# Retention's last gate behind the first Fourier projection, Fourier's second gate between later branches, and the first modulation in eight pieces

## The chip, the cores and the metric

The kernel runs on one core of one Trainium2 chip. The metric is the device time of one execution in microseconds (us). The engines are PE (TensorE, matrix products), DVE (VectorE), ACT (ScalarE), POOL (GpSimd) and SP (which only issues transfers); PEld is PE's weight load, and a q behind a name (SPq, ACTq) is the queue from which that engine issues transfers.

## The reference, cut to what matters

Two layers of a trunk on 640 tokens (512 of a sample, 128 of a prompt) of width 1024. Each layer modulates its input, projects it once into many strips, runs three branches, gates each with a SiLU of its own strip of the projection, multiplies each by a branch weight, merges the three under sigmoid gates, and projects back.

```python
mod = silu(cvec) @ w_mod + b_mod
shift, scale, gate = split(mod, 3)
h = rms_norm(x, norm_g) * (1 + scale) + shift
rq, rk, rv, rz, q_lat, kv_lat, k_r, mz, fu, fz, gl = split(h @ w_in)
o_r = head_norm(retention(rq, rk, rv))        # 4 heads of 128
o_m = mla_attend(q_lat, kv_lat, k_r)          # 8 heads
o_f = fft2(fu).real                           # 4 groups of 128
branches = stack([o_r * silu(rz), o_m * silu(mz), o_f * silu(fz)])
proj = einsum(branches, w_branch)             # 3 x (512 -> 1024)
merged = sum(proj * sigmoid(gl))              # gl: 3 x 1024 columns
x = x + gate * (merged @ w_out)
```

## The kernel before, in words

Hidden values lie transposed: channels on partitions, the 640 tokens along the row, so one strip of 128 channels is a tile of 128x640. Each float32 operand is split into a high and a low part (`split`, L78 the cast on ACT, L74 the difference on DVE or POOL), and each product takes three passes (high by high, low by high, high by low). `hh` and `hl` are the two parts of h; `wh` and `wl` those of a weight.

**Order.** A tile scheduler puts the instructions of each engine into one fixed order; the place of a statement in the code is its priority. At run time every engine works its list strictly in that order, and an instruction that waits holds up all behind it on that engine.

**Start** (L1150 to L1190). SP issues the loads: x in five tiles, then the columns of the modulation weight `w_mod` and four pieces of the weight of the latents (`lat_w`, tiles `raw` of 128x2x384) in the order of the string `m2 w0 m0 w1 n6 n2 n7 n3 w2 w3`: m is a block of 512 columns in two transfers of 1 MB, n one of 256 columns in two of 0.5 MB, all in the ring `mraw` of five buffers of 1 MB. PE multiplies a block by the conditioning (`fill`, L187), ACT copies the result (L192), PE turns it over (L196), and it lands in `modT`, the scale and shift. x is squared in 20 pieces on ACT (L1168), summed and rooted on DVE and POOL, spread (L245), turned over (L1178), scaled (L1181, `xr`), modulated (L1187) and split into `hh` and `hl`, for the eight channel blocks d = 0 to 7. Blocks 0 to 3 need m2 and m0, 4 and 5 need n6 and n2, 6 and 7 need n7 and n3. The latents (384 columns, 120 matmuls) come first, then the keys' and values' latents (288 columns, 120 matmuls).

**Retention** (L690 to L835). Head by head: scores, mixing, `norm(hd)` and `gate(hd)`. `norm` copies the head's output to a tile `of` (L782), turns it over (five transposes, L787), takes mean and variance (DVE L789, L790), a power on POOL (L793, L794), the offset on DVE (L795), and normalises on ACT (L798). `gate` turns it back (five transposes, L807) and multiplies by the SiLU of strip rz (DVE L808). The strips of rz are computed by `Filler` (L319, 48 matmuls a strip, with tanh L321 and DVE L322), which other work pours between its own instructions; `finish` pours what is left of a strip. `norm(3)` and `gate(3)` stand at the end.

**Fourier** (L838 to L945). `sums(0)` to `sums(3)` form sums of token halves of h (`hx`, `hq0h` and so on, the operands of `seven` below), using the tiles `of` as scratch. `project(g)` makes two groups of the projection fu in five products of 24 matmuls (`sm`, L85 to L87), each copied by ACT (`un`, L855, from a ring of `sm` banks). Transforms follow, and gates: `z0`, `z1` for the groups 0 and 1 (`fourier_gate`, L954), and behind them, in the branch part, groups 2 and 3 by one `seven`.

**Branches** (L1192 to L1310). `seven` computes 256 output columns with seven half-sized products (84 matmuls of 320 columns, L1109) instead of eight, from sums of inputs and sums of weights. The loop `n` takes the branches in the order attention, retention, Fourier; in each, i = 0 to 3 takes 256 columns of the sigmoid gate (a `seven` from `hq`), then of the branch product (a `seven` from `bq`, or `four`). The operands `bq0` to `bq9` and `bql` are parts of the branch's input, made by `branch_sums` with sums on DVE (L1010 to L1013) and splits, at the ticks of the first gate's `seven` or at once behind it. `bql` lies in the memory of the Fourier tiles `of`, so those are stored to `ofd` first and loaded back into `or` for the third branch; `om` holds attention's output and then scratch. `tick` also steers `steps`, the loads (`mraw`, by ACTq) and products of the next modulation.

## Time and profile before

| | us |
|---|---|
| device time, median of 3 runs (1477.54 to 1480.52) | 1479.51 |
| the profiled execution's own time | 1482.52 |
| its span in the trace | 1480.7 |
| PE busy in the span | 1416.7 (96%) |
| DVE busy | 1024.6 (69%) |
| ACT busy | 758.5 (51%) |
| POOL busy | 241.8 (16%) |

Times in the rows are microseconds from the start of the span. A row of the timeline gives the start, the busy time, the engine, the line and operation with the tile it writes and those it reads, how many follow in a row, and in brackets the idle time of the engine before it and what released it. Matmuls overlap, so a matmul of 0.31 us may be followed by the next one 0.15 us later. PEclk is the clock that TensorE was granted, 1.00 for 2.4 GHz; a stretch below 1.00 ran partly at 1.2 GHz. The chain that ended last is 72% PE, 13% DVE, 6% transfers, 4% ACT.

### The profile page before, as it was taken

What the parts mean: (1) busy time and instruction counts of PE and PEld (TensorE: products, weight loads), DVE (VectorE), ACT (ScalarE), POOL (GpSimd) and SP (SyncE); (2) the same over time, 40 slices, a digit from 0 to 9 for tenths busy, and PEclk for the clock granted to TensorE, in tenths of its full rate; (3) what the DMA queues carried; (4) which work ended last, traced back from release to release, by engine and by line L of the source; (5) the groups of instructions that cost most, each with busy time, mean ns of one, the idle gap of its engine ahead of it and who ended that gap; (6) DMA issues with size and microseconds to landing.
All of it is one profiled execution on the core that took longest, in us unless ns stands there. A gap on an engine that the chain in (4) does not pass through costs nothing.

```text
span 1480.7 us, 25121 instructions
## 1 busy us (share of the span) xinstructions
PE 1416.7 (96%) x9761; PEld 1346.9 (91%) x9761; DVE 1024.6 (69%) x1894; ACT 758.5 (51%) x1635; POOL 241.8 (16%) x227
## 2 busy tenths in 40 slices
PE   5999999999999999999999999999999999999997
PEld 3989989988897898999999899899889889999997
DVE  5367776667886686698573777765759768779843
ACT  6357666544544453455344566664545445445542
POOL 1220100301102111122312100021110112112240
PEclk9999999999999999999999999999999999999999
DMA  9520002421326464133532100042222424333342
GB/s 330 164 76 1 15 15 78 121 76 41 93 90 189 143 192 122 51 86 93 171 104 83 34 15 15 15 137 75 74 72 65 154 82 116 95 82 86 90 125 86
DMA packets 173735, 138.91 MB, mean 94 GB/s; under 512 B 8240, under 2 KB 164528, under 8 KB 173616
## 3 DMA queue, kind: packets, MB, share of 16 engines
q1 hardware_dynamic: 155568, 120.16, 28.0%
q10 hardware_dynamic: 18048, 17.15, 3.7%
q8 instruction: 77, 1.26, 0.4%
q14 instruction: 42, 0.34, 0.1%
HBM read 125.98 MB, written 11.30 MB: 93 GB/s over the span
## 4 chain that ended last, share of the span: by engine, by line
PE 72%; DVE 13%; DMA 6%; ACT 4%; issue 4%; POOL 1%; SPq 0%; POOLq 0%; DVEq 0%; ACTq 0%
PE bank L1109 25%; PE sm L85 5%; PE sm L87 5%; PE sm L86 5%; PE bank L1080 4%; PE big L513 4%; PE fill L319 3%; PE big L269 3%; PE sm L319 3%; PE sm L534 3%; DVE wl L74 2%; PE sm L526 2%; DMA mraw<-in_w_mod 2%; PE fill L187 1%; DMA raw<-in_w_in 1%
## 5 line engine op out<-in xcount | busy, mean ns | idle before, releaser
L74 DVE TENSOR_TENSOR wl<-raw,wh 128x1024 fp32r<-128x1024 f32 (+5 forms) x146 | 156.2, 1072 | 92.1 <-ACT wh L78 45.1
L78 ACT CAST wh<-raw 128x1024 fp32r<-128x1024 f32 (+5 forms) x126 | 104.4, 832 | 79.0 <-DMA raw<-in_w_in 18.1
L85 PE MATMUL sm<-wh,hh 128*128 128x256 f32 (+2 forms) x456 | 134.7, 296 | 0.4 <-DVE vl L74 0.4
L87 PE MATMUL sm<-wh,hl 128*128 128x256 f32 (+2 forms) x456 | 133.9, 294 | 0.9 <-DVE hl L74 0.9
L1109 PE MATMUL bank<-hh,wh 128*128 128x320 f32 x416 | 130.7, 316 | 4.0 <-ACT tg L1125 2.9
L86 PE MATMUL sm<-wl,hh 128*128 128x256 f32 (+2 forms) x456 | 134.5, 295 | 0.0
L1109 PE MATMUL bank<-hl,wh 128*128 128x320 f32 x416 | 129.5, 312 | 0.0
L1109 PE MATMUL bank<-hh,wl 128*128 128x320 f32 x416 | 127.8, 313 | 0.0
L74 POOL TENSOR_TENSOR wl<-raw,wh 128x1024 fp32r<-128x1024 f32 (+1 forms) x32 | 67.6, 2112 | 296.9 <-ACT wh L78 221.2
L74 POOL TENSOR_TENSOR wl<-st,wh 128x512 fp32r<-128x512 f32 x26 | 39.2, 1508 | 324.2 <-ACT wh L78 302.1
L85 PEld LDWEIGHTS sm<-wh,hh 128*128 128x128 f32 x456 | 88.2, 194 | 1.5 <-DVE vl L74 0.8
L87 PEld LDWEIGHTS sm<-wh,hl 128*128 128x128 f32 x456 | 88.0, 193 | 1.4 <-DVE hl L74 1.4
L86 PEld LDWEIGHTS sm<-wl,hh 128*128 128x128 f32 x456 | 88.4, 194 | 0.1
L1109 PEld LDWEIGHTS bank<-hh,wh 128*128 128x128 f32 x416 | 79.1, 190 | 9.9 <-ACT tg L1125 3.6
L1109 PEld LDWEIGHTS bank<-hl,wh 128*128 128x128 f32 x416 | 79.2, 190 | 0.0
L1109 PEld LDWEIGHTS bank<-hh,wl 128*128 128x128 f32 x416 | 78.7, 191 | 0.4 <-DVE raw L1025 0.4
L74 DVE TENSOR_TENSOR ptl<-sm,pth 128x384 fp32r<-128x384 f32 x128 | 67.4, 549 | 14.4 <-ACT pth L78 13.3
L1109 PE MATMUL bank<-bq,wh 128*128 128x320 f32 x320 | 72.1, 311 | 0.0
L78 ACT CAST pth<-sm 128x384 fp32r<-128x384 f32 x128 | 57.5, 480 | 24.1 <-PE sm L526 23.3
L78 ACT CAST wh<-st 128x512 fp32r<-128x512 f32 x68 | 39.7, 618 | 53.0 <-PE bank L1109 53.0
L640 DVE TENSOR_REDUCE nm<-big 128x1 f32<-128x768 f32 x64 | 60.7, 948 | 2.7 <-PE big L513 2.4
L74 DVE TENSOR_TENSOR wl<-st,wh 128x512 fp32r<-128x512 f32 x42 | 41.2, 980 | 30.2 <-ACT wh L78 27.7
(579 smaller groups left out, 4546.3 us busy)
## 6 DMA issues: line engine op xcount, KB each, us to landing
raw<-in_w_in SPq DMA_DIRECT2D x96, 512.0 KB, 4.0
mraw<-in_w_mod ACTq DMA_DIRECT2D x32, 512.0 KB, 4.3
raw<-in_w_branch SPq DMA_DIRECT2D x24, 512.0 KB, 3.6
raw<-in_w_out SPq DMA_DIRECT2D x16, 512.0 KB, 4.5
mraw<-in_w_mod SPq DMA_DIRECT2D x4, 1024.0 KB, 11.7
mraw<-in_w_mod SPq DMA_DIRECT2D x8, 512.0 KB, 8.3
raw<-in_w_in SPq DMA_DIRECT2D x8, 384.0 KB, 5.9
om<-xd SPq DMA_DIRECT2D x16, 192.0 KB, 3.1
```

Of the source, the lines that this page charges most:

```text
L74: eng.tensor_tensor(lo, src, hi.bitcast(F32), op=ALU.subtract)
L78: ACT.copy(hi, src)
L85: PE.matmul(out, ah, bh, start=first, stop=False)
L86: PE.matmul(out, ah, bl, start=False, stop=False)
L87: return PE.matmul(out, al, bh, start=False, stop=last)
L269: PE.matmul(ps[:, 512 * h:512 * h + 320], ws[a][:, k, :], xs[b][k][:, 320 * h:320 * h + 320], start=(first and k == 0 and i == 0), stop=(l ...
L319: PE.matmul(ps, w[a][:, k, :], (hh, hl)[b][k][:, hs], start=(k == 0 and i == 0), stop=(k == NK - 1 and i == 2))
L513: PE.matmul(S[:, 512 * h:512 * h + 384], qT[hd][a][:, t * P:(t + 1) * P], (kth, ktl)[b][hd % 3][:, 384 * h:384 * h + 384], start=(i == 0), ...
L534: PE.matmul(po[:, :256], vt[hd // 4][kt][:, hd % 4, :], pts[hd, qb][b][kt // 3][:, kt % 3, :], start=(kt == 0 and b == 0), stop=(kt == 5 a ...
L640: DVE.tensor_reduce(nm, Sv, axis=AX.XY if len(Sv.shape) == 3 else AX.X, op=ALU.max, negate=True)
L1080: PE.matmul(A, ws[u][:, k, j * P:(j + 1) * P], xs[k][v][:, h, :], start=(k == 0 and i == 0), stop=(k == 3 and i == 2))
L1109: PE.matmul(ps, w[u], x[v], start=(first and k == 0 and j == 0), stop=(k == n - 1 and j == 2), skip_group_check=True)
```

## The change

1. `retention` no longer runs `gate(3)` but returns it. `fourier` runs `sums(0)`, `project(0)`, then that gate, then `sums(1)` to `sums(3)`; before, the gate stood first, then the four sums, then `project(0)`. Head 3's normalised output lies in the last of the four `of` tiles, which `sums(1)` uses.
2. The gates of Fourier's groups 2 and 3 (columns `C_FZ+256`, one `seven` with its weights, two tanh, two SiLU products, two gates) move from behind the Fourier branch into the loop, ahead of n = 2. They are now applied in `or`, where the Fourier tiles have been loaded back. The weights that were fetched ahead for it (`w0`) are now those of the first gate of n = 0. All four stores to `ofd` are issued at the first tick of n = 0 (before: two behind Fourier, two behind the gates).
3. The first modulation comes in eight blocks of 256 columns, in the order 4, 0, w0, 5, 1, w1, 6, 2, w2, 7, 3, w3, in a ring of ten buffers of 0.5 MB, and the modulation of blocks d = 2i, 2i+1 is written right behind its two blocks. x is squared in five pieces of 1024 with the sum accumulated, ahead of the loads in the code.
4. In the branches the parts of `bq` change place in the list (`bql` serves the products 3 and 6, before 4 and 6), at n = 0 a part is made at every tick (before at every second), and the scratch tiles of n = 2 swap parity.

```diff
--- before.py
+++ after.py
@@ -832,10 +832,10 @@
         for p in todo:
             mix(*p)
         norm(3)
-        gate(3)
-
-
-    def fourier(l, fp, of, sums, wgp):
+        return lambda: gate(3)
+
+
+    def fourier(l, fp, of, sums, wgp, lastgate):
         def table(name, src, a, n):
             raw = fp.tile([P, a, n], F32, name="traw", tag="traw", bufs=1)
             nc.sync.dma_start(raw, src)
@@ -915,9 +915,11 @@
             split(upc[0][:, g, :], upc[1][:, g, :], Up[:, 0:P], scale=1.0 / 128)
             split(ups[0][:, g, :], ups[1][:, g, :], Up[:, P:256], scale=-1.0 / 128)
 
-        for k in range(4):
+        sums(0)
+        project(0)
+        lastgate()
+        for k in range(1, 4):
             sums(k)
-        project(0)
         teo = [table(f"te{i}", A["k_dft"][i].rearrange("(a p) n -> p a n", p=P), 2, 256) for i in range(2)]
         tp_ = table("tpr", A["k_dftp"].unsqueeze(1), 1, 256)
         cf = table("tcf", A["k_dftf"].unsqueeze(1), 1, 256)
@@ -938,7 +940,7 @@
         along_c(3)
         fourier_prompt(of, cf, upc, ups)
         wz, z1 = wload(rows(A["w_in"][l], 0, NK, C_FZ + P, P), NK, P, DVE), []
-        ws = gl_weights(wgp, l, C_FZ + 256, lambda: z1.append(silu2(l, C_FZ + P, wz)))
+        ws = gl_weights(wgp, l, C_GL + D, lambda: z1.append(silu2(l, C_FZ + P, wz)))
         fourier_gate(of, 0, z0)
         return ws, fourier_gate(of, 1, z1[0])
 
@@ -994,7 +996,7 @@
         B = lambda i, c: sv[:, i, :, HALF[c]]
         t = [gp.tile([P, 2, 320], F32R, name=f"bq{i}", tag=f"bq{i}", bufs=1) for i in range(10)]
         x = [spare[:, i, :].rearrange("p (k n) -> p k n", k=2) for i in range(4)]
-        t = t[:8] + x[:2] + t[8:] + x[2:]
+        t = t[:6] + x[:2] + t[6:] + x[2:]
 
         def place(i, x, eng):
             hi, lo = t[2 * i:2 * i + 2]
@@ -1149,25 +1151,17 @@
 
     po1 = sm()
 
-    def start(order):
-        for o in order.split():
-            if o[0] == "w":
-                first.append(lat_w(0, int(o[1])))
-            else:
-                n, b = {"m": 512, "n": 256}[o[0]], int(o[1])
-                for j in range(0, NK, 4):
-                    mod_use(0, b, j, mod_load(0, b, j, prep, n, 512, 4, 5, nc.sync), n, 4, po1[:, 2 * (b * n // P):])
+    def scaled(d):
+        v = xrs[d]
+        for c, s_ in ((0, slice(0, T)), (1, slice(T, TT))):
+            DVE.tensor_scalar(v[:, s_], v[:, s_], modT[0][:, 8 + d, c:c + 1], modT[0][:, d, c:c + 1], op0=ALU.mult, op1=ALU.add)
+        split(hh[d], hl[d], v, leng=POOL if d % 2 else DVE)
 
     for t in range(NT):
         nc.sync.dma_start(xn[t], A["x_sample"][0, t * P:(t + 1) * P, :] if t < 4 else A["x_prompt"][0])
-    start("m2 w0 m0 w1 n6 n2 n7 n3 w2 w3")
     rin = prep.tile([P, NT], F32, name="rin")
-    rq4 = prep.tile([P, NT, 4], F32, name="rq4")
     for t in range(NT):
-        for j in range(4):
-            ACT.activation(omt[:, j, 0:256], xn[t][:, 256 * j:256 * j + 256], AF.Square, scale=D ** -0.5,
-                           accum_out=rq4[:, t, j:j + 1])
-    DVE.tensor_reduce(rin, rq4, axis=AX.X, op=ALU.add)
+        ACT.activation(omt.rearrange("p w n -> p (w n)")[:, 0:D], xn[t], AF.Square, scale=D ** -0.5, accum_out=rin[:, t:t + 1])
     POOL.tensor_scalar(rin, rin, EPS, None, op0=ALU.add)
     POOL.tensor_tensor(rin, rin, mhalf[:, 0:NT], op=ALU.pow)
     R, _ = bcast(prep, rin, 0, NT)
@@ -1181,11 +1175,13 @@
         DVE.tensor_tensor(xr, ps[:, :TT], R, op=ALU.mult)
         xts.append(xt)
         xrs.append(xr)
-    for d in range(NK):
-        v = xrs[d]
-        for c, s_ in ((0, slice(0, T)), (1, slice(T, TT))):
-            DVE.tensor_scalar(v[:, s_], v[:, s_], modT[0][:, 8 + d, c:c + 1], modT[0][:, d, c:c + 1], op0=ALU.mult, op1=ALU.add)
-        split(hh[d], hl[d], v, leng=POOL if d % 2 else DVE)
+    for i in range(4):
+        for b in (4 + i, i):
+            for j in range(0, NK, 4):
+                mod_use(0, b, j, mod_load(0, b, j, prep, 256, 256, 4, 10, nc.sync), 256, 4, po1[:, 4 * b:])
+        first.append(lat_w(0, i))
+        for d in (2 * i, 2 * i + 1):
+            scaled(d)
     xstore = [nc.sync.dma_start(xd[0][d], xts[d]) for d in range(NK)]
     pre.close()
 
@@ -1202,18 +1198,16 @@
         orr = [ort[:, w, :] for w in range(4)]
         off = [oft[:, w, :] for w in range(4)]
         with ExitStack() as s:
-            retention(l, pool(s, f"re{l}"), orr, off)
+            lastgate = retention(l, pool(s, f"re{l}"), orr, off)
         s3 = ExitStack()
         hqp = pool(s3, f"hq{l}")
         wgp = pool(s3, f"wg{l}")
         with ExitStack() as sx:
             sums, close, hq = hidden_sums(hqp, pool(sx, f"hx{l}"), off)
             with ExitStack() as s:
-                w0, gated = fourier(l, pool(s, f"fo{l}"), off, sums, wgp)
+                w0, gated = fourier(l, pool(s, f"fo{l}"), off, sums, wgp, lastgate)
             close()
         ofd = dp.tile([P, 4, TT], F32, name=f"ofd{l}")
-        for w in range(2):
-            nc.sync.dma_start(ofd[:, w, :], oft[:, w, :])
         mgp = pool(s3, f"mg{l}")
         mg = [mgp.tile([P, TT], F32, name=f"mg{d}") for d in range(NK)]
         mh, ml = hh, hl
@@ -1226,16 +1220,13 @@
             steps = mod_steps(blocks, gp)
             next(steps)
             a, b = HALF
-            zs = [fl.tile([P, TT], F32, name="tg", tag="th", bufs=2) for _ in range(2)]
 
             def fourier_done(j):
-                z, m, o = zs[j], mg[j], off[j + 2]
+                z, m, o = om[2 + j], om[j], ort[:, 2 + j, :]
                 ACT.activation(m, z, AF.Tanh, scale=0.5)
                 DVE.scalar_tensor_tensor(m, m, 1.0, z, op0=ALU.add, op1=ALU.mult)
-                fourier_gate(off, j + 2, m)
-                nc.sync.dma_start(ofd[:, j + 2, :], o)
-
-            seven(w0, hq, *zs, lambda ps: ACT.copy(zs[0][:, b], ps), fourier_done, lambda i: None)
+                DVE.scalar_tensor_tensor(o, o, 0.5, m, op0=ALU.mult, op1=ALU.mult)
+
             bql = rp2.tile([P, 4, TT], F32R, name="bql", tag="of", bufs=1)
 
             def merge(d0, d1, hs=slice(0, TT)):
@@ -1253,7 +1244,10 @@
                 def tick(i):
                     if i in (3, 6):
                         next(steps, None)
-                    if i % 2 and len(bq) < np_:
+                    if not n and not bq and not i:
+                        for w in (2, 3, 0, 1):
+                            nc.sync.dma_start(ofd[:, w, :], oft[:, w, :])
+                    if (i % 2 or not n) and len(bq) < np_:
                         with tc.issue_after(gated.ins):
                             bq.append(next(parts))
 
@@ -1278,15 +1272,17 @@
             for n, (idx, src, tmp) in enumerate(((1, omt, None), (0, ort, om), (2, ort, om))):
                 if n:
                     flush()
+                if n == 2:
+                    seven(gl_weights(wgp, l, C_FZ + 256), hq, om[2], om[3], lambda ps: ACT.copy(om[2][:, b], ps), fourier_done, lambda i: None)
                 parts = branch_split(gp, src) if n == 1 else branch_sums(gp, src, bql)
                 np_ = 4 if n == 1 else 7
                 bq = []
                 for i in range(4):
-                    if n and i % 2 == 0:
+                    if n and i % 2 == n - 1:
                         y2 = tmp[2:4]
                     else:
                         y2 = [fl.tile([P, TT], F32, name="tg", tag="th", bufs=2) for _ in range(2)]
-                    seven(gl_weights(wgp, l, C_GL + D * idx + 256 * i), hq, *y2, *gates(y2, n, bq, parts, np_))
+                    seven(w0 if not (n or i) else gl_weights(wgp, l, C_GL + D * idx + 256 * i), hq, *y2, *gates(y2, n, bq, parts, np_))
                     if n == 2 and i == 3:
                         merge(0, 4)
                     if i == 0:
```

SP, the loads at the start, before (`mraw` 1 MB or 0.5 MB, `raw` 0.39 MB):

```order
L175 DMA mraw_188<-in_w_mod 128x4x512
L175 DMA mraw_195<-in_w_mod 128x4x512
L92 DMA raw_208<-in_w_in 128x2x384
L175 DMA mraw_214<-in_w_mod 128x4x512
L175 DMA mraw_221<-in_w_mod 128x4x512
L92 DMA raw_233<-in_w_in 128x2x384
L175 DMA mraw_239<-in_w_mod 128x4x256
L175 DMA mraw_246<-in_w_mod 128x4x256
L92 DMA raw_309<-in_w_in 128x2x384
L175 DMA mraw_257<-in_w_mod 128x4x256
```

and now:

```order
L175 DMA mraw_284<-in_w_mod 128x4x256
L175 DMA mraw_291<-in_w_mod 128x4x256
L175 DMA mraw_302<-in_w_mod 128x4x256
L175 DMA mraw_309<-in_w_mod 128x4x256
L92 DMA raw_319<-in_w_in 128x2x384
L175 DMA mraw_333<-in_w_mod 128x4x256
L175 DMA mraw_340<-in_w_mod 128x4x256
L175 DMA mraw_351<-in_w_mod 128x4x256
L175 DMA mraw_358<-in_w_mod 128x4x256
L92 DMA raw_368<-in_w_in 128x2x384
L175 DMA mraw_382<-in_w_mod 128x4x256
L175 DMA mraw_389<-in_w_mod 128x4x256
```

The large transfers are gone; two blocks of 256 columns stand ahead of each piece of the latents' weight.

ACT in the first layer, from the normalisation of head 3 (L798) to the copies of `project(0)` (L855), before (`wh` and `th` belong to the gates' strips and weights):

```order
L321 ACTIVATE th_4267<-fill_4268 128x320
L782 COPY of_2986<-big_4098 128x640
L78 CAST wh_4607<-raw_4605 128x1024
L321 ACTIVATE th_4267<-fill_4295 128x320
L798 ACTIVATE of_2986<-big_4233,nm5_4252,rs5_4251 128x128 x5
L855 COPY un_4404<-sm_4417 128x256
L855 COPY un_4404<-sm_4443 128x256
L855 COPY un_4404<-sm_4469 128x256
L78 CAST te0h_4552<-traw_4550 128x512
```

and now:

```order
L782 COPY of_3000<-big_4112 128x640
L321 ACTIVATE th_4466<-fill_4467 128x320
L798 ACTIVATE of_3000<-big_4247,nm5_4266,rs5_4265 128x128 x5
L78 CAST wh_4621<-raw_4619 128x1024
L321 ACTIVATE th_4466<-fill_4494 128x320
L855 COPY un_4314<-sm_4327 128x256
L855 COPY un_4314<-sm_4353 128x256
L855 COPY un_4314<-sm_4379 128x256
L78 CAST te0h_4566<-traw_4564 128x512
```

The weight cast and the tanh stand behind L798 instead of ahead of it, and ahead of the three copies.

PE at the same place, around the last gate's transposes (L807), before (`sm_4469` and `sm_4495` are the third and fourth product of `project(0)`):

```order
L85 MATMUL sm_4469<-wh_4413,hh7_156 128x256
L86 MATMUL sm_4469<-wl_4414,hh7_156 128x256
L87 MATMUL sm_4469<-wh_4413,hl7_164 128x256
L807 MATMUL big_4322<-ident_72,of_2986 128x128 x5
L85 MATMUL sm_4495<-wh_4407,hh0_149 128x256
L86 MATMUL sm_4495<-wl_4408,hh0_149 128x256
```

and now (`fill` is the gate strip's second half, `sm_4405` the fourth product of `project(0)`):

```order
L319 MATMUL fill_4494<-hh7_156,wh_4462 128x320
L319 MATMUL fill_4494<-hl7_164,wh_4462 128x320
L319 MATMUL fill_4494<-hh7_156,wl_4463 128x320
L807 MATMUL big_4521<-ident_72,of_3000 128x128 x5
L85 MATMUL sm_4405<-wh_4317,hh0_149 128x256
L86 MATMUL sm_4405<-wl_4318,hh0_149 128x256
```

The gate's transposes stand behind the strip's matmuls and ahead of the fourth product. Between L787 and L807 now stand 24 matmuls of the strip, before 1 of the strip and 23 of the third product.

DVE at the entry of n = 2 in the first layer, before (`bq` are the operands of the third branch, `wl` weights, `tg` and `om` results of `seven`):

```order
L1022 TENSOR_TENSOR st_7272<-raw2_7264 128x512
L74 TENSOR_TENSOR bq1_7052<-or_2985,bq0_7051 128x640
L74 TENSOR_TENSOR bq5_7056<-or_2985,bq4_7055 128x640
L1010 TENSOR_TENSOR or_2985<-or_2985 128x2x320
L74 TENSOR_TENSOR wl_7086<-raw_7061,wh_7085 128x1024
L74 TENSOR_TENSOR bq7_7058<-or_2985,bq6_7057 128x640
L1013 TENSOR_TENSOR or_2985<-or_2985 128x2x320
L74 TENSOR_TENSOR bq3_7054<-or_2985,bq2_7053 128x640
```

and now (`or` holds the Fourier tiles):

```order
L1227 SCALAR_TENSOR_TENSOR om_165<-om_165 128x640
L1115 TENSOR_TENSOR om_165<-bank_7004,om_165 128x320
L1228 SCALAR_TENSOR_TENSOR or_2999<-or_2999,om_165 128x640
L1227 SCALAR_TENSOR_TENSOR om_165<-om_165 128x640
L1228 SCALAR_TENSOR_TENSOR or_2999<-or_2999,om_165 128x640
L74 TENSOR_TENSOR wl_7279<-raw_7274,wh_7278 128x1024
L1115 TENSOR_TENSOR tg_7042<-bank_7148,tg_7042 128x320
L74 TENSOR_TENSOR bq9_7040<-or_2999,bq8_7039 128x640
L1026 TENSOR_TENSOR raw_7274<-raw_7274,raw2_7276 128x512
L1027 TENSOR_TENSOR raw_7274<-raw_7274,st_7285 128x512
L74 TENSOR_TENSOR bq5_7036<-or_2999,bq4_7035 128x640
L1010 TENSOR_TENSOR or_2999<-or_2999 128x2x320
```

The two SiLU products and the two gates stand ahead of the first operands of the branch, which before came with no gate ahead.

## Rows read from the trace of the kernel before

**Rows 1.** The page: PE's busy time.

```profile
PE 1416.7 (96%) x9761; PEld 1346.9 (91%) x9761; DVE 1024.6 (69%) x1894; ACT 758.5 (51%) x1635; POOL 241.8 (16%) x227
```

**Rows 2.** Waits of PE: line, waited for, us in total, times, longest.

```profile
PE fill L187 <- DMA mraw<-in_w_mod: 13.4, 4, 12.4
PE big L807 <- ACT of L798: 5.3, 2, 2.6
PE bank L1109 <- ACT bql L78: 4.1, 2, 2.1
PE bank L1109 <- ACT tg L1125: 2.9, 2, 2.4
```

**Rows 3.** Windows: busy us by engine, PEclk, DMA share, GB/s; around PE's waits.

```profile
380.00:385.00 5.00, 4.96 (x25) 4.46 (x26) 3.97 (x8) 3.82 (x11) 0.61 (x1) 0.67 0.84 218
465.00:470.00 5.00, 2.94 (x14) 1.90 (x15) 3.20 (x6) 3.96 (x7) 0.17 (x1) 0.71 0.81 261
1190.00:1195.00 5.00, 5.00 (x24) 5.00 (x25) 5.00 (x8) 2.47 (x6) 1.82 (x1) 0.66 0.02 6
```

**Rows 4.** Windows as above, of the start.

```profile
17.00:22.00 5.00, 4.99 (x31) 3.12 (x27) 1.69 (x2) 2.98 (x5) 0.29 (x1) 1.00 1.05 386
27.00:32.00 5.00, 3.78 (x39) 2.50 (x37) 4.89 (x12) 3.64 (x8) 0.00 (x0) 1.00 1.10 357
61.00:77.00 16.00, 16.00 (x118) 16.00 (x117) 2.47 (x7) 10.48 (x30) 7.46 (x18) 1.00 0.16 46
```

**Rows 5.** Timeline of the start.

```profile
7.17 0.42 ACT L1168 ACTIVATE om<-xn 128x256 f32<-128x256 f32 x1 [2.49 <-DMA xn<-in_x_sample]
...
39.25 0.33 PE L86 MATMUL sm<-wl,hh 128*128 128x384 f32 x1
...
39.94 0.34 PE L87 MATMUL sm<-wh,hl 128*128 128x384 f32 x1
...
77.14 0.60 PE L403 MATMUL sm<-ident,latq 128*128 128x128 f32 x4
```

**Rows 6.** Timeline of the last norm and gate of retention, first layer.

```profile
373.05 0.71 PE L787 MATMUL big<-ident,of 128*128 128x128 f32 x5
373.25 1.05 ACT L78 CAST wh<-raw 128x1024 fp32r<-128x1024 f32 x1 [2.98 <-PE fill L319]
...
374.21 0.43 ACT L321 ACTIVATE th<-fill 128x320 f32<-128x320 f32 x1
...
374.88 1.20 DVE L74 TENSOR_TENSOR wl<-raw,wh 128x1024 fp32r<-128x1024 f32 x1
...
378.76 1.85 ACT L798 ACTIVATE of<-big,nm,rs 128x128 f32<-128x128 f32 x5 [4.13 <-DVE nm L795]
...
379.27 1.72 PE L807 MATMUL big<-ident,of 128*128 128x128 f32 x5 [2.63 <-ACT of L798]
...
380.49 0.94 ACT L855 COPY un<-sm 128x256 f32<-128x256 f32 x3
...
380.93 0.39 PE L85 MATMUL sm<-wh,hh 128*128 128x256 f32 x1
```

**Rows 7.** Timeline of n = 0: first layer, and one row of the second.

```profile
435.61 0.82 DVE L954 SCALAR_TENSOR_TENSOR of<-of,th 128x640 f32<-128x640 f32 x1
...
458.14 0.81 DVE L1234 SCALAR_TENSOR_TENSOR mg<-mg,tg 128x640 f32<-128x640 f32 x1
...
459.27 0.81 DVE L954 SCALAR_TENSOR_TENSOR of<-of,mg 128x640 f32<-128x640 f32 x1
...
460.11 0.34 SPq L1236 DMA_DIRECT2D ofd<-of  x1
...
466.04 0.72 ACT L78 CAST bql<-om 128x640 fp32r<-128x640 f32 x1 [3.78 <-DMA ofd<-of]
...
466.80 0.83 DVE L74 TENSOR_TENSOR bql<-om,bql 128x640 fp32r<-128x640 f32 x1 [6.16 <-ACT bql L78]
...
1189.16 1.35 ACT L78 CAST bql<-om 128x640 fp32r<-128x640 f32 x2 [3.08 <-DMA ofd<-of]
```

## Prediction

> **What bounds the kernel now.** I read the page's busy times first: PE is busy for 1416.7 us of the span of 1480.7 [rows 1]. That leaves 64 us in which PE stands idle. The change adds no matmul and removes none that matters, so it can only win or lose in these 64 us and in the stretches where PE's clock is low. The second view is therefore the list of PE's waits [rows 2]. The first row there, 13.4 us for `mraw`, is the start: 12.4 of it is one wait, for the first block. The next three rows are the places that the change touches: 5.3 us before the gates' transposes L807 (two waits, one in each layer, the longest 2.6), 4.1 us for `bql` (two), and 2.9 us for `tg` (two, longest 2.4, nearly all in the second layer). The third view is the windows around these waits. Behind each PE's granted clock is under 1.00: 0.67 in 380 to 385, 0.71 in 465 to 470, 0.66 in 1190 to 1195 [rows 3]. A five-microsecond window at 0.67 does the work of 3.35 us, so each wait of two microseconds or more costs a further 1.65 us or so of slow matmuls. The fourth view is the timeline of each place, to see what ends the wait.
>
> **The start.** PE's last matmul of both latent phases ends at 77.14 [rows 5], and what counts is how much earlier that is. A 384-column matmul follows the next in 0.173 us (four of them from 39.25 to 39.94 [rows 5]); in the 288-column phase 118 instructions fill 16.00 us [rows 4], 0.136 each, 0.133 without the few others. Before, the first latents can start only when the 512-column blocks m2 and m0 have come through, and PE then has 120 x 0.173 + 120 x 0.133 = 36.8 us of latents left, and the other blocks' products among them. Now blocks 4 and 0 alone release d = 0 and 1, and half the latents can be done while the rest is loaded. What ends the wait then is the transfers. 2.6 MB of x, sixteen pieces of `w_mod` (8.4 MB) and four of the latents' weight (1.6 MB) are needed, 12.6 MB; the first 0.5 MB has landed at 7.17 [rows 5]. The other 12.1 MB take 31.3 us at the 386 GB/s of the window 17 to 22 and 33.9 us at the 357 GB/s of 27 to 32 [rows 4], so the last piece lands between 38.5 and 41.1; I take 39.3. The last thing in the queue is now the latents' fourth weight piece. Its cast on ACT, about 0.8 us by the 1.05 of the 1024-wide one [rows 6] scaled to 768 columns, lets PE go on at about 40.2 to 41. By the order of the changed program some 60 latent matmuls are left by then and all 120 of the second phase, with 0.8 of others: 60 x 0.173 + 120 x 0.133 + 0.8 = 27.2 us. From 40.6 that ends at 67.8, against 77.1: -9.3. PE waits for pieces between 36 and 40, and such a wait costs a low clock like those of [rows 3], +1.65. Sum **-7.5**. The ends: -12 if the last piece lands at 38.5 and the clock holds, -4 if it lands at 41.1 and PE has less done before. The squares in five pieces finish earlier than the twenty; that is not on this path, because the transfers end last.
>
> The rows show what halving a piece costs in rate: 386 GB/s with 1 MB pieces, 357 GB/s with 0.5 MB pieces [rows 4], and 4.2 MB go from the first kind to the second: 11.7 instead of 10.9 us, +0.8, which lies within my 39.3. The Trainium skill, page "DMA: Bandwidth & Descriptors", section "Bandwidth", speaks against the smaller pieces: it asks for transfers of at least 1 MiB for 75% of the peak, and its fit puts about 2 us on each transfer whatever its size; four more transfers in a row would by that be an estimate of 8 us, and the start's sum +0.5. The trace does not agree so far: the rate fell by 7.5%, not by half.
>
> **Retention's last gate, two layers.** Before: from L787 at 373.05 to L798 at 378.76 run statistics, power and offset, with a weight's low part of 1.20 us in the middle of the statistics; L807 starts at 379.27 after 2.63 idle, and takes 1.72 because each transpose waits for its piece of L798's 1.85 [rows 6]. With the clock that is 2 x (2.63 + 1.65) = 8.6 us. The change puts the gate further back in the code, but the order shows that its transposes still stand one strip's half (24 matmuls) behind L787. A 320-column matmul takes 0.144 us (0.173 x 320/384), so these are 3.5 us, and with L787's 0.5 PE has work for 4.0. The chain loses the low part and DVE's strip product, so L798 starts about 4.8 after L787 instead of 5.7; L807 0.5 later: PE waits 1.3 instead of 2.63. But on ACT a cast of 1.05 and a tanh of 0.43 now stand between L798 and the copies `un`; before, both were done while ACT waited for L798 (373.25, 374.21 [rows 6]). The fourth product of the projection stands behind L807 on PE and needs the bank that the first copy frees: before it started at 380.93, 2.2 after L798 began. Now the copy ends 1.85 + 1.05 + 0.43 + 0.31 = 3.64 after L798 began, and PE is free 0.5 + 1.72 = 2.2 after it: a new wait of 1.4. Together 2.7 against 2.63, within 3 us, so I expect the clock to fall as before. Sum **0**; ends -8.6 (both waits covered) and +4 (the cast waits for its weight's transfer). `sums(1)` to `sums(3)`, queued behind the gate on DVE, have ten microseconds until `seven` needs them.
>
> **The stores and the operands at n = 0.** Before, `bql` is cast at 466.04 after ACT has waited 3.78 for the stores to `ofd`, the last of which is issued at 460.11 behind the second Fourier gate (459.27); in the second layer the same cast waits 3.08 and starts at 1189.16 [rows 7]. PE waits 2.1 and 2.0 for it, and 2.4 for `tg` [rows 2]; with the clock at 0.71, 0.66 and a third such fall this is (2.1 + 1.45) + (2.0 + 1.7 + 2.4 + 1.6) = 11.3. Now the four stores are issued when the gate of group 1 is done, which before ran from 435.61 to 436.43 [rows 7]; the last store before took 5.9 us from its issue to the cast, so the cast waits no longer than to about 443. But the whole `seven` of the Fourier gate, 84 x 0.144 = 12.1 us of PE work, no longer stands between the Fourier branch and this place: the operands, five pairs of cast and low part (0.72 and 0.83 each [rows 7]) and four sums, are wanted 12 us sooner, and DVE is the engine that makes them. Going through PE's and DVE's order with these durations, PE waits 0.7 at the products 5 or 6 and 2 to 3 at the second: 2.3 and a fall of the clock, 3.9 a layer. Sum 7.8 - 11.3 = **-3.5**; ends -11 (all covered) and +2.
>
> **The Fourier gate at n = 2.** The trace has nothing of this at its new place. Behind its `seven` come a copy and a tanh on ACT (about 0.8 by the 0.43 of a half strip), L1234 of 0.81 and L954 of 0.81 on DVE [rows 6, 7], for two groups. Before the last two operands of that branch can be cast, 3.2 us pass from the `seven`'s last product, and cast and low part make it 4.8. PE has the next gate's `seven` (12.1 us) as cover, but its queue holds the branch's products between the pieces of that `seven`, and behind these two gates DVE has the sums, low parts and weights of [rows 7] in line. Going through the order I get waits of 0.5, 1.3, 0.85 and 0.2, 2.9 a layer, none long enough for the clock. Sum **+5.7**; ends 0 (the `seven` covers all) and 4.8 + 1.65 = 6.4 a layer, +12.8. The rest of the change (places in the operand list, parity of the scratch) has the same operations: 0.
>
> **Sum.** -7.5 + 0 - 3.5 + 5.7 = -5.3. The profiled execution took 1482.52, 3.0 above the median of 1479.51 of the runs shown: 1477.2 for a profiled execution, **1474.2** for the median.
>
> **The rivals.**
> A, the waits go away. The code reads as if each wait named in [rows 2] had lost its cause: the start -7.5, the gates -8.6, n = 0 -11.3, n = 2 nothing because of a `seven`'s cover. That is -27.4, 1452. For it: every one of these waits has its releaser moved. Against it: the order, which leaves the transposes 24 matmuls behind L787 and puts ACT's cast ahead of the copies. In full 3%, in two of the four places (1458 to 1466) 15%.
> B, slower. The Fourier gates ahead of n = 2 hold DVE so long that PE waits twice for 2 us or more, once for the operands of the last two groups and once for what these delay: 4.8 and two falls of the clock, 8.1 a layer, +16.2 instead of +5.7. That gives +5.2, 1484.7. It decides from about 7 us a layer. For it: DVE is full around operand splits (5.00 of 5 in 1190 to 1195 [rows 3]). Against it: 12.1 us of cover. 14%.
> C, the start gains nothing. If the sixteen smaller pieces run under 300 GB/s (a window with two queues at work has 261 [rows 3]), the last lands after 47 and the gain is gone: 1481.7, no change. The skill's rule above is this rival's other form. 8%.
> D, the change does not do what it says: excluded by the order, which shows all three moves; 0%.
>
> **How the numbers follow.** The forecast has 60%, and its own range is 1467 to 1482. About 0.2% (3 us) is what a measurement of this kernel can tell from no change: below 1476.5 is faster, above 1482.5 slower. Of the forecast's 60% about 42 are faster, 17 within, 1 slower; A adds 18 to faster; B is slower but for 2 within; C 5 within and 1 each to the sides, rounded: faster 0.62, same 0.23, slower 0.15. The range from 1464 to 1483 leaves out most of A and B.
>
> **What would show it.** In the changed profile: the first phase's end (the transposes of `latq`) near 68 instead of 77.14; L807's idle time near 1.3, and a wait of the fourth projection product for `un` of about 1.4 behind it; no wait of a `bql` cast for `ofd`; a clock near 0.7 at 380 to 385 minus the start's gain; new waits of PE for `bq` at n = 2, 3 us a layer. The prediction is wrong if L807's place shows neither wait (faster by up to 8.6), if the waits at n = 2 come to more than 7 a layer (slower), or if the last of `w_mod` lands after 43 (the start's gain halved).

## The result, and the profile after

The changed kernel takes 1492.71 us (median of 4 runs, 1491.37 to 1493.91) against 1480.01 before: a ratio of 1.0085, interval 1.0069 to 1.0101. It is 0.85% slower, where 1474.2 was forecast. The profiled execution took 1493.13, with a span of 1491.3 instead of 1480.7.

The page has PE busy 5.4 us longer than before [rows 1], for a span 10.6 longer.

```profile
span 1491.3 us, 25154 instructions
...
PE 1422.1 (95%) x9793; PEld 1348.3 (90%) x9793; DVE 1026.5 (69%) x1896; ACT 760.9 (51%) x1607; POOL 237.1 (16%) x227
```

The list of PE's waits (line, waited for, us in total, times, longest) answers [rows 2]:

```profile
PE fill L187 <- DVE dec L168: 11.0, 1, 11.0
PE bank L1111 <- DVE bq L74: 5.6, 2, 2.8
...
PE bank L1111 <- ACT om L1133: 5.0, 4, 2.3
PE bank L1111 <- ACT tg L1127: 3.1, 2, 1.7
...
PE sm L85 <- ACT un L855: 2.4, 2, 1.2
```

Two of the four waits of [rows 2] are gone, for L798 and for `bql`. The one at the start is 11.0 instead of 12.4 and is now put down to DVE's `dec`, and the one for `tg` has stayed. New are those for `bq` and for `om`, and a smaller one for `un`. The windows around them (busy us by engine, PEclk, DMA share, GB/s) answer [rows 3]: the clock now falls behind the new waits. It does not fall more often, though: the mean granted clock of the profiled execution is 0.992, where it was 0.990 before.

```profile
640.00:645.00 5.00, 4.51 (x21) 4.25 (x20) 5.00 (x11) 2.62 (x4) 0.00 (x0) 0.67 0.40 106
...
1105.00:1110.00 5.00, 3.85 (x20) 3.86 (x21) 5.00 (x8) 3.80 (x10) 1.50 (x1) 0.66 0.30 69
...
1350.00:1355.00 5.00, 3.05 (x11) 2.86 (x12) 5.00 (x8) 1.73 (x3) 1.22 (x1) 0.66 0.41 105
...
1415.00:1420.00 5.00, 4.24 (x17) 4.24 (x18) 3.14 (x5) 1.34 (x3) 3.06 (x2) 0.66 0.44 129
```

**Where the time went.** I compared the moments at which both traces pass the same point, and took off 12.3 us where one `seven` has changed sides. The start gives 4.2 us. From there to the first Fourier gate 1.0 is lost again in the first layer, and 1.9 in the second (2.4 lost behind the last norm, 0.5 gained ahead of it). Between the Fourier gates and the end of n = 1 the kernel gains 2.4 and 4.8. From there to the next layer, or the end of PE's work, it loses 9.1 and 10.2. So n = 2 alone costs 19, and n = 2 is what has to be explained. Measured as one stretch, from PE's last matmul of n = 1 to the last of the last `seven` of n = 2, it takes 100.6 and 100.5 instead of 78.4 and 78.3: 9.9 a layer more than the 12.3 of the `seven` that moved there. In this stretch PE waits for 7.3 and 6.6 instead of 0.6 a layer, and the lower clock behind these waits costs another 1.7 and 2.8.

The entry of n = 2 in the first layer, timeline:

```profile
629.48 1.30 POOL L74 TENSOR_TENSOR w<-raw,w 128x512 fp32r<-128x512 f32 x1 [4.70 <-ACT w L78]
629.49 0.48 DVE L1115 TENSOR_TENSOR om<-bank,om 128x320 f32<-128x320 f32 x1
629.89 1.57 DVE L1228 SCALAR_TENSOR_TENSOR or<-or,om 128x640 f32<-128x640 f32 x1
...
635.55 1.51 POOL L74 TENSOR_TENSOR wl<-st,wh 128x512 fp32r<-128x512 f32 x1 [4.78 <-ACT wh L78]
...
635.83 1.77 DVE L1027 TENSOR_TENSOR raw<-raw,st 128x512 f32<-128x512 f32 x1
...
637.29 1.44 POOL L74 TENSOR_TENSOR w<-raw,w 128x512 fp32r<-128x512 f32 x1 [0.23 <-ACT w L78]
637.53 1.88 DVE L74 TENSOR_TENSOR bq<-or,bq 128x640 fp32r<-128x640 f32 x1
...
639.46 0.41 PE L1111 MATMUL bank<-bq,wh 128*128 128x320 f32 x1 [2.80 <-DVE bq L74]
```

PE waits 2.80 for DVE's low part of `bq`. That instruction took 0.83 in [rows 7] and takes 1.88 here; the one ahead of it takes 0.68 elsewhere and 1.77 here. Each began while POOL was at work, and ended 0.54 and 0.68 after POOL's instruction (the second: 637.29 + 1.44 + 0.68 = 639.41 = 637.53 + 1.88), which is its own time less some 0.14. DVE was not working so long; it waited for POOL. One of the moved gate's own two-operand products, L1228, is held in the same way (1.57 instead of 0.82). L1115 beside the same POOL instruction, with one operand in a PSUM bank, is not (0.48). In the second layer the wait for `bq` is 2.80 again. The Trainium skill, page "SBUF — State Buffer", section "SBUF: two separate sides", states this as a rule: DVE and GpSimd share a pair of ports that one of them holds for a whole instruction, if DVE's has two inputs in SBUF and GpSimd's reads SBUF, and the other is blocked until then. The trace agrees, with 1.88 for 0.82.

DVE was held up before the change as well. Over n = 2 its instructions ran 9.9 and 10.3 us beyond their own times before, and 12.9 and 10.6 now. What is new is that PE waits for it.

The end of n = 2, first layer, and a few rows of the second:

```profile
698.75 4.10 SPq L92 DMA_DIRECT2D raw<-in_w_out  x2
...
700.06 2.40 POOL L74 TENSOR_TENSOR wl<-raw,wh 128x1024 fp32r<-128x1024 f32 x1 [10.58 <-ACT wh L78]
...
700.18 3.69 DVE L82 SCALAR_TENSOR_TENSOR hl<-mg,hh 128x640 fp32r<-128x640 f32 x2
...
702.93 1.05 ACT L78 CAST wh<-raw 128x1024 fp32r<-128x1024 f32 x1 [2.36 <-DMA raw<-in_w_out]
703.88 0.42 ACT L1133 COPY om<-bank 128x320 f32<-128x320 f32 x1
...
704.35 0.56 PE L1111 MATMUL bank<-bq,wh 128*128 128x320 f32 x2 [2.27 <-ACT om L1133]
...
1411.57 1.55 DVE L82 SCALAR_TENSOR_TENSOR hl<-mg,hh 128x640 fp32r<-128x640 f32 x2
...
1414.34 1.05 ACT L78 CAST wh<-raw 128x1024 fp32r<-128x1024 f32 x1 [2.09 <-DMA raw<-in_w_out]
1415.29 0.42 ACT L1133 COPY om<-bank 128x320 f32<-128x320 f32 x1
...
1415.76 0.56 PE L1111 MATMUL bank<-bq,wh 128*128 128x320 f32 x2 [2.28 <-ACT om L1133]
```

In the first layer two instructions of DVE take 3.69 beside POOL's 2.40. That is not what PE waits for: in the second layer the same pair takes 1.55, and PE waits 2.28 all the same. In both layers the copy that frees the bank stands in ACT's order behind the cast of a weight of the output projection, and that cast waits for its transfer, which was issued at 698.75 and landed some 4.1 us later. So the end's wait is one of ACT's order. No run moves this cast alone; it is read from the traces.

### The profile page after: what moved, and what is told of

It reads as the page before. It is cut to its first block, busy times and chain, and to the rows that moved or that the text cites. A ratio compares the mean times of both kernels' runs of the same rounds, so it can differ in the third digit from the quotient of the medians.

```text
span 1491.3 us, 25154 instructions
## 1 busy us (share of the span) xinstructions
PE 1422.1 (95%) x9793; PEld 1348.3 (90%) x9793; DVE 1026.5 (69%) x1896; ACT 760.9 (51%) x1607; POOL 237.1 (16%) x227
## 4 chain that ended last, share of the span: by engine, by line
PE 74%; DVE 13%; ACT 4%; issue 4%; DMA 3%; POOL 1%; SPq 0%; ACTq 0%; POOLq 0%; DVEq 0%
PE bank L1111 23%; PE sm L85 6%; PE sm L86 6%; PE sm L87 6%; PE big L269 4%; PE bank L1082 4%; PE big L513 4%; PE fill L319 3%; PE sm L319 3%; PE sm L534 2%; PE fill L187 2%; DVE wl L74 2%; PE sm L526 2%; DMA raw<-in_w_in 1%; PE big L411 1%
## 5 line engine op out<-in xcount | busy, mean ns | idle before, releaser
L74 POOL TENSOR_TENSOR wl<-raw,wh 128x1024 fp32r<-128x1024 f32 (+1 forms) x32 | 63.3, 1978 | 335.9 <-ACT wh L78 236.8
L1111 PEld LDWEIGHTS bank<-hh,wh 128*128 128x128 f32 x416 | 78.7, 190 | 12.8 <-issue 4.9
L74 DVE TENSOR_TENSOR wl<-st,wh 128x512 fp32r<-128x512 f32 x42 | 49.3, 1174 | 39.0 <-ACT wh L78 36.5
L1111 PEld LDWEIGHTS bank<-bq,wh 128*128 128x128 f32 x320 | 53.5, 189 | 16.8 <-DVE bq L74 6.1
```

The source lines that it names most:

```text
L74: eng.tensor_tensor(lo, src, hi.bitcast(F32), op=ALU.subtract)
L1111: PE.matmul(ps, w[u], x[v], start=(first and k == 0 and j == 0), stop=(k == n - 1 and j == 2), skip_group_check=True)
```

## Experiments

All times are medians; ratios are against the kernel before, run beside each (1478.3 to 1479.4 in the several sessions, 1480.0 beside the changed kernel). So a difference between kernels of different sessions is uncertain by 1 to 2 us. Where a stretch is given, it is from the one profiled execution of the kernel.

**e1_start**: the third part alone, as in the diff of the change.

> Only the third part of the change (first modulation in eight blocks, squares in five pieces), all else as before. In the trace of the changed kernel the second latent phase ended at 72.94 instead of 77.14. Theory (the start gives 4 us and keeps it): 4 us less than before. Rival (what the start gives is lost again by the first retention heads, where the changed kernel stood 3.2 ahead): 3 us less or under.

Measured 1471.35, ratio 0.9953 (0.9940 to 0.9966): 8.1 less. The two profiled executions differ by 11.2. In this one the second latent phase ends at 72.6, 4.5 earlier, and n = 0 is shorter by 2.5 in the first layer and 3.1 in the second. There PE no longer waits for `bql`, though the stores to `ofd` stand where they stood; why is not shown. Neither expectation had it right. The forecast's -7.5 for the start comes near only together with these gains at another place.

**e2_gate**: the first part alone.

> Only the first part (retention's last gate behind the first Fourier projection). Theory (the wait before L807 is exchanged for one for the copies un, plus small waits in the Fourier part, with the clock fall kept in one layer): between 1 us less and 3 us more than before. Rival (the gate's wait goes): 4 to 8 us less.

Measured 1483.73, ratio 1.0025 (1.0010 to 1.0041): 4.3 more, a little over the theory's end. The rival falls.

**e3_four**: the second and fourth part.

> Only the second part with the fourth (Fourier's second gate ahead of n = 2, operand places, ticks, scratch parity). Theory (this part carries the loss: n = 2 costs some 10 us a layer, n = 0 gives 2.5 and 4.9 back): 12 to 14 us more than before. Rival (the loss comes of the other parts shifting the queues): within 4 us of before.

Measured 1497.15, ratio 1.0126 (1.0111 to 1.0142): 17.7 more. The loss is here, more of it than the theory had. In its trace the stretch n = 2 takes 100.8 and 100.7, as in the changed kernel.

**e4_n1**: the changed kernel with the gate's `seven` at another place.

```diff
-                if n == 2:
-                    seven(gl_weights(wgp, l, C_FZ + 256), hq, om[2], om[3], ...)
...
+                    if n == 1 and i == 3:
+                        seven(gl_weights(wgp, l, C_FZ + 256), hq, om[2], om[3], ...)
```

> The changed kernel with one thing moved: the seven of Fourier's second gate stands ahead of the last gate (i = 3) of n = 1 instead of ahead of n = 2. Theory (the loss is that the gated strips come too late for the operands of n = 2): the waits for bq at the entry of n = 2 go and the kernel takes 12 to 20 us less than the changed one, 1473 to 1481. Rival (the loss is from the operand places, the ticks and the scratch parity, which stay): within 4 us of the changed kernel, 1489 to 1496.

Measured 1478.42, ratio 0.9997 (0.9985 to 1.0009): 14.3 less than the changed kernel. The operand places, ticks and parity are unchanged in it, so the place of the gate ahead of n = 2 makes the loss, and not those. The stretch n = 2 takes 78.7 and 77.4 in its trace, as before the change.

**e5_start_n1**: as e4_n1, without the first part.

> The third part (start), and the second and fourth with Fourier's second gate ahead of the last gate of n = 1 instead of ahead of n = 2; retention's last gate as before the change. Theory (the parts add up: start -8, retention's gate +4, and moving the gate to n = 1 leaves only the gain at n = 0): 1468 to 1475. Rival (the gate's place in n = 1 takes back what n = 0 gives, the start alone stays): 1471 or more, no better than the start alone.

Measured 1476.61, ratio 0.9982 (0.9972 to 0.9991). The start alone has 1471.35, so the rival holds: at n = 1 the gate takes some 5 us more than n = 0 gives.

**e6_parity**: the changed kernel with the scratch of n = 2 as before.

```diff
-                    if n and i % 2 == n - 1:
+                    if n and i % 2 == 0:
...
+                    zs[:] = [fl.tile([P, TT], F32, name="tg", tag="th", bufs=2) for _ in range(2)]
```

> The changed kernel with the scratch parity of n = 2 as before the change (the third branch's even steps in om, odd steps in the tg ring; the gate's two strips in the tg ring). In the changed trace PE waits 2.3 us near the end of n = 2 in each layer for a copy into om that DVE's queue frees late. Theory (that wait comes of the swapped parity): it goes, with its fall of the clock, 4 to 8 us less than the changed kernel, 1485 to 1489. Rival (the end of n = 2 only inherits the delay of its entry): within 2 us, 1491 to 1495.

Measured 1496.15, ratio 1.0120 (1.0102 to 1.0137), 3.4 more than the changed kernel, which is neither expectation. The theory falls, and with it parity as the cause of the wait at the end of n = 2: it was 2.0 and 1.4 there, and the one for `bq` had grown to 4.3 in the first layer.

**e7_nopool**: the changed kernel, POOL's low parts replaced at the entry of n = 2.

```diff
+        if quiet and eng is POOL:
+            POOL.memset(lo.bitcast(F32), 0.0)
+            return
         eng.tensor_tensor(lo, src, hi.bitcast(F32), op=ALU.subtract)
...
+                    quiet.append(1)
+                    if n == 2 and i == 1:
+                        quiet.clear()
```

> The changed kernel, but from the entry of n = 2 to its second step the low parts of weights that POOL makes are filled with zero instead (seven instructions a layer are left out of the arithmetic, so these products are less exact). In the changed trace DVE's low part of bq took 1.88 instead of 0.82, and a difference of weights 1.77 instead of 0.68, while POOL ran such an instruction. Theory (DVE and POOL hold each other up there, and that makes the 2.8 us wait for bq): the two are 0.8 and 0.7 again, the wait falls to 0.7 or less in both layers, 4 to 8 us less than the changed kernel, 1485 to 1489. Rival (DVE's queue of gates, sums and splits is too long by itself): the wait stays above 1.7, within 3 us of the changed kernel.

Measured 1488.58, ratio 1.0069 (1.0055 to 1.0083): 4.1 less than the changed kernel by the medians, 2.4 by the ratios. The same place in its timeline:

```profile
634.73 0.53 POOL L77 MEMSET wl<- 128x512 f32 x1 [5.25 <-PE bank L1116]
...
634.88 0.69 DVE L1031 TENSOR_TENSOR raw<-raw,raw 128x512 f32<-128x512 f32 x1
635.48 0.69 DVE L1032 TENSOR_TENSOR raw<-raw,st 128x512 f32<-128x512 f32 x1
...
636.09 0.82 DVE L79 TENSOR_TENSOR bq<-or,bq 128x640 fp32r<-128x640 f32 x1
...
636.69 0.53 POOL L77 MEMSET w<- 128x512 f32 x1 [1.44 <-PE bank L1116]
...
636.96 0.41 PE L1116 MATMUL bank<-bq,wh 128*128 128x320 f32 x1 [0.39 <-DVE bq L79]
```

DVE's two instructions are 0.69 and 0.82 again and the wait is 0.39, in the second layer 0.43. The theory holds for the entry; the order of DVE's work hardly differs. The stretch n = 2 takes 97.0 and 97.4 in this trace, 3.6 and 3.1 less than in the changed kernel's. The wait at the end stays (up to 2.6).

**e8_un_dve**: the first part, and the copies of the first projection on DVE.

```diff
-                    ACT.copy(un[t], ps)
+                    (ACT.copy if ch else DVE.tensor_copy)(un[t], ps)
```

> Only the first part (retention's last gate), and the copies of the first Fourier projection done by DVE instead of ACT. Theory (the wait behind the gate's transposes is ACT's order: cast and tanh stand ahead of the copies): the waits of 1.2 for the copies go, 2 to 6 us less than with the first part alone, 1478 to 1482. Rival (the bank is held by something else, or DVE's own queue is no faster): within 2 us of the first part alone, 1482 to 1486.

Measured 1484.10, ratio 1.0031 (1.0014 to 1.0047), no better than e2_gate. The wait for `un` is gone from PE's list, but others have grown:

```profile
PE sm L87 <- DVE fw L74: 2.7, 2, 1.4
...
PE sm L85 <- ACT fh L78: 2.2, 2, 1.1
```

The rival holds: DVE's queue is no better place for the copies.

**e9_quiet_end**: as e7_nopool, but nothing clears `quiet`. The edit so goes further than the expectation says: from the entry of n = 2 in the first layer on, all of POOL's low parts are left out up to the end of the program, those of the second layer's other stages too.

> The changed kernel with the low parts of weights that POOL makes filled with zero from the entry of n = 2 to the last weight of the output projection (left out of the arithmetic, both layers). With only the entry so, the wait for bq fell from 2.8 to 0.4, but PE still waited 2.0 to 2.6 near the end of n = 2, where two of DVE's instructions took 3.69 together beside a POOL one of 2.40. Theory (the end is the same contention): DVE's two take 1.6, the end's wait falls under 1, 2 to 6 us less than with the entry alone, 1482 to 1486. Rival (the end's wait is DVE's order): the wait stays near 2, within 2 us of the run with the entry alone, 1487 to 1490.

Measured 1476.97, ratio 0.9983 (0.9971 to 0.9994): 11.6 less than with the entry alone, and 15.7 less than the changed kernel. In its trace DVE's pair at the end takes 1.55:

```profile
693.88 1.55 DVE L87 SCALAR_TENSOR_TENSOR hl<-mg,hh 128x640 fp32r<-128x640 f32 x2
...
694.97 0.41 PE L1116 MATMUL bank<-hh,wh 128*128 128x320 f32 x1 [0.97 <-ACT om L1138]
...
698.46 0.42 ACT L1138 COPY om<-bank 128x320 f32<-128x320 f32 x1
...
702.24 1.05 ACT L83 CAST wh<-raw 128x1024 fp32r<-128x1024 f32 x1 [3.36 <-DMA raw<-in_w_out]
```

That does not show the theory. The changed kernel's second layer has 1.55 for this pair too, and waited 2.28. What differs is ACT's order, which changed with the edit: the copy now stands ahead of the cast that waits for the transfer. The stretch n = 2 takes 94.5 and 94.8, 2.5 and 2.6 less than in e7_nopool. The rest of the 11.6 lies in other stages, which the edit also reaches, and goes with a higher granted clock (0.993 to 0.997 against 0.991 to 0.994). Neither expectation came true: the time lies below both, and neither cause is shown.

**e10_no_four**: the first and third part.

> The first and third part (retention's gate, start) without the moved Fourier gate. Theory (the parts add up, start -8, gate +4, and the moved Fourier gate is all of the loss): 1473 to 1478. Rival (the start's gain depends on the rest): 1480 or more.

Measured 1479.27, ratio 1.0006 (0.9989 to 1.0022), between the two expectations. The start and the gate do not quite add up (8.1 less and 4.3 more would be 1475): with the start ahead of it the gate costs 8. Its 12 runs lie between 1474 and 1487, so this is known to some 2 us only.

**e11_late_norm**: as e10_no_four, and the normalisation L798 of head 3 moves with the gate.

```diff
-            for t in range(NT):
-                ACT.activation(nn[:, t * P:(t + 1) * P], pn[:, t * P:(t + 1) * P], AF.Identity, ...)
-            outp[hd] = nn
+            outp[hd] = of
+            def apply():
+                for t in range(NT):
+                    ACT.activation(of[:, t * P:(t + 1) * P], pn[:, t * P:(t + 1) * P], AF.Identity, ...)
+            if hd == 3:
+                return apply
+            apply()
...
-        norm(3)
-        return lambda: gate(3)
+        late = norm(3)
+        return lambda: (late(), gate(3))
```

> As the run without the moved Fourier gate, and the last normalisation of retention on ACT (the five instructions ahead of the gate's transposes) is written behind the first Fourier projection too, with the gate. In the order of the program ACT then makes the three copies of the projection ahead of the normalisation, and PE has 72 matmuls instead of 24 between the two groups of transposes. Theory (the gate brought nothing because ACT's normalisation stood ahead of the copies, so that the projection's fourth product could not fill the gap): neither the wait of 2.6 nor that of 1.2 is left, 6 to 11 us less than the run without the moved Fourier gate, 1463 to 1469. Rival (the projection's products are then missing later, where PE waits for Fourier's transforms): within 3 us of that run.

Measured 1465.92, ratio 0.9908 (0.9895 to 0.9921): 13.4 less than e10_no_four, 13.4 less than before, and the fastest of all. Its timeline at the place of [rows 6]:

```profile
368.58 0.92 ACT L859 COPY un<-sm 128x256 f32<-128x256 f32 x3
...
372.46 1.86 ACT L799 ACTIVATE of<-big,nm,rs 128x128 f32<-128x128 f32 x5 [2.95 <-DVE nm L794]
...
378.64 0.71 PE L811 MATMUL big<-ident,of 128*128 128x128 f32 x5
```

The copies now stand ahead of the normalisation, in ACT's idle time. The fourth and fifth product of the projection fill the gap, and the transposes wait for nothing and take 0.71, where they took 1.72. The theory holds at this place: from L787 of head 3 to the first Fourier gate 3.3 and 4.1 us less pass than in e10_no_four, 7.4 together, within its 6 to 11. The other 6 of the 13.4 lie elsewhere in the program, and why is open.

**e12_before_quiet**: a control, the kernel before with POOL's low parts left out from the entry of n = 2 to the last weight of the output projection. Here `quiet` is cleared, so the edit reaches less than that of e9_quiet_end.

> A control: the kernel before, with the same low parts of weights filled with zero by POOL as in the last run of that kind (from the entry of n = 2 to the last weight of the output projection, left out of the arithmetic). Theory (before the change PE did not wait for DVE there, so POOL's instructions beside DVE's cost it little): 0 to 3 us less than before, 1476 to 1480, and the difference of 11 to 16 us that the same edit made in the changed kernel is what the move of the gate lost to them. Rival (the edit gains as much without the move, since POOL held DVE up there already): 8 us or more less, 1471 or under.

Measured 1477.32, ratio 0.9985 (0.9972 to 0.9998): about 2 less. The difference to the 15.7 of e9_quiet_end is no measure of the move, since the two edits are not the same. The stretch n = 2, where they are, can be compared: here it takes 78.3 and 78.3, against 78.4 and 78.3 without the edit, although DVE is busy for 62.6 us in it instead of 70.9. In the changed kernel the edit takes off 6.1 and 5.7. So before the move POOL beside DVE cost PE nothing there, and behind it up to 6 us a layer, of which the entry's 3.6 and 3.1 (e7_nopool) go with POOL's instructions there; the rest goes with ACT's changed order at the end as well.

## Why the prediction was wrong, step by step

- **The start** (-7.5): the part alone gave -8.1, but that it comes so near is luck, because at the start itself only 4.2 us were gained (4.5 in e1_start). The latents end at 72.94, not near 68. The last piece landed at 41.9, where 39.3 was taken, but PE is never idle for 0.4 us from 14.27 on, so it did not wait for it. The term that was too small is the work left. At 40.6 PE still had 73 latent matmuls of the first phase ahead of it, where 60 were reckoned with, and the last products of the blocks with their turning over took 3.7 us, where 0.8 stood for them. The rest of the 8.1 was gained elsewhere, in n = 0 above all. Rival C is refuted, since the rate was near the 357 that the forecast took:

```profile
17.00:22.00 5.00, 5.00 (x41) 3.26 (x40) 2.02 (x5) 3.31 (x6) 0.00 (x0) 1.00 1.09 353
...
72.94 0.49 PE L403 MATMUL sm<-ident,latq 128*128 128x128 f32 x3
```

353 GB/s stand against 386 in [rows 4]. The Trainium skill, page "DMA: Bandwidth & Descriptors", has the fit with 2 us a transfer in its section "Anatomy of one DMA — SWDGE (gpsimd) path", for transfers issued from GpSimd; here SP issues them. The prediction's estimate of 8 us by it does not come out: the start ends 4.2 earlier with four more transfers, not later.

- **Retention's gate** (0): the mechanism as told, an exchange of waits:

```profile
373.79 1.86 ACT L798 ACTIVATE of<-big,nm,rs 128x128 f32<-128x128 f32 x5 [3.87 <-DVE nm L795]
...
374.30 1.73 PE L807 MATMUL big<-ident,of 128*128 128x128 f32 x5
...
375.52 1.06 ACT L78 CAST wh<-raw 128x1024 fp32r<-128x1024 f32 x1
...
376.45 0.47 ACT L321 ACTIVATE th<-fill 128x320 f32<-128x320 f32 x1
376.78 0.95 ACT L855 COPY un<-sm 128x256 f32<-128x256 f32 x3
...
377.24 0.38 PE L85 MATMUL sm<-wh,hh 128*128 128x256 f32 x1 [1.21 <-ACT un L855]
```

Of the two forecast waits of 1.3 and 1.4 the first is not there, since the chain ran in 4.5 us instead of 4.8, and the second is 1.21. Yet the part costs 4.3 alone and 8 beside the start. New waits farther on in Fourier's part (for `fh`, `ups` and the gate strip) account for part of it, and the clock fell in one layer of this execution, not in the other. The wait for `un` by itself is not the cause: e8_un_dve removes it and is no faster. With the normalisation moved along, the loss goes (e11_late_norm). What makes up the rest of it stays open.

- **n = 0** (-3.5): the gain was 2.4 + 4.8 = 7.2, with no wait for the stores. Part of it (2.5 and 3.1) came with the start alone in e1_start, so it is not all the stores' earlier place:

```profile
437.95 0.72 ACT L78 CAST bql<-om 128x640 fp32r<-128x640 f32 x1
...
440.32 0.41 PE L1111 MATMUL bank<-hh,wh 128*128 128x320 f32 x1 [1.40 <-ACT tg L1127]
```

One wait of 1.40, without a fall of the clock, is what remains of the 2.3 and a fall that were feared.

- **n = 2** (+5.7): this step failed, a term of 19 us in its place. The order on PE and DVE was read rightly, but the instructions were given the durations that they have alone, and ACT's order at the end of n = 2 was left out. At the entry two of DVE's instructions beside POOL took over twice that, and PE waited 2.80 a layer for the operand that they make; with memsets in place of POOL's subtractions the wait is 0.4 and n = 2 is 3.6 and 3.1 shorter (e7_nopool). At the end PE waited 2.27 and 2.28 for a copy that stands on ACT behind a cast whose weight had not landed. So two waits over 2 us a layer came where four short ones were forecast, and falls of the clock behind them. This is rival B in shape, which was given 14% and 8.1 a layer; 9.1 and 10.2 were measured. Its reason, DVE's full queue, is only half of the first wait, and has no part in the second. PE's waits in this stretch, 7.3 and 6.6, lie at the 7 that the prediction named as the sign of a slower kernel. Rival B's total of 1484.7 was too low, mostly because the start and the gate gave less than forecast. The trace of the kernel before had shown how POOL holds DVE up, at a place where nobody waited for it:

```profile
701.80 2.39 POOL L74 TENSOR_TENSOR wl<-raw,wh 128x1024 fp32r<-128x1024 f32 x1 [0.26 <-ACT wh L78]
701.86 3.01 DVE L1271 TENSOR_TENSOR mg<-mg,om 128x640 f32<-128x640 f32 x1
```

The second takes 0.81 without POOL. Looking for such rows on both engines, ahead of a change that puts more on DVE, would have moved the forecast to the other side.

- **Sum.** Forecast -5.3 against the profiled execution before. By the runs of the parts: -8.1 + 4.3 + 17.7 = 13.9; measured 12.7. That these agree is partly luck, since two of the parts do not add up: the start and the gate together measured nothing (1479.27 in e10_no_four), not -3.8.

## What to carry to other kernels

When work is moved onto an engine's critical stretch, take its durations from rows where the neighbours run as they will there: in these traces a DVE instruction with two operands in SBUF, beside a POOL one that reads SBUF, ended its own time less some 0.14 us after POOL's end. Look along each engine's order, too, for a copy that frees a bank and stands behind an instruction that waits for a transfer: here that was worth a wait of 2.3 us a layer. When a scheduler orders each engine, moving a late step is of use only if all that it depends on moves with it: the gate alone exchanged one wait for another, and with the normalisation moved along the kernel became 13 us faster, 7.4 of them at that place. Of a change in parts, time the parts: one of these was worth 8 us and was buried under another's 18. And a control has to make the same edit: where it reaches less, only the stretch that both reach can be compared.

## What the hardware showed that I had not expected

POOL's memset beside DVE's two-input instruction did not hold DVE up (0.69 beside one of 0.53, at 634.73 and 634.88 in e7_nopool), where its subtraction did. And kernels with waits of a little over a microsecond spread more: the twelve runs of e8_un_dve go from 1474.04 at a mean granted clock of 0.997 to 1490.77 at 0.985, while the start alone keeps within 1470.70 to 1473.30 at 0.992 to 0.994. Their times go with the granted clock. Within one execution the clock fell behind such a wait at one place and not at another: behind the same 1.21 of the wait for `un` it stayed at 1.00 in the changed kernel's first layer and fell to 0.66 in its second.
